# Rotary steps on VectorE straight from PSUM sums, and the indexer's columns as two held chunks and 80 float32 columns

## The chip, the cores and the metric

The kernel runs on one core of a Trainium2 chip. The time is the device time of one execution in microseconds (us); a comparison is made against runs of the kernel before on the same chip. PE is TensorE, DVE is VectorE, ACT is ScalarE, POOL is GpSimd, SP is the queue that issues the weight loads.

## The reference

One decoder layer on 256 rows of 2048 float32 values. What the change touches is the part from the first norm to the two attentions:

```python
h = _rmsnorm(x, g_pre_mix[l]) * (1.0 + sc1) + sh1        # sc1, sh1 = sections of silu(c) @ w_ada + b_ada
proj = h @ w_in[l]                                       # (256, 2048) @ (2048, 11344)
p_moba, p_dsa, p_qi, p_ki, p_wi, ga, gb = jnp.split(proj, split_pts, axis=-1)
q_idx = _rope(p_qi.reshape(B, T, IDX_HEADS, IDX_DIM))    # 16 heads x 64
k_idx = _rope(p_ki[:, :, None, :])[:, :, 0, :]           # 64 columns; p_wi has 16
ya = _moba_attention(_rope(qa), _rope(ka), va)...        # 8 heads x 128, causal softmax at this length
yb = _dsa_attention(_rope(qb), _rope(kb), vb, q_idx, k_idx, p_wi)...
# inside _dsa_attention: rel = relu(q_idx . k_idx); score = sum_h p_wi * rel * scale; keep the 64 largest per row
# _rope: [x1*cos - x2*sin, x2*cos + x1*sin] on the two halves of each head
```

Behind it come the gates, the two output projections, `w_o`, a second norm and a squared-ReLU MLP of width 8192; the change leaves these alone.

## The kernel before

**Tiles.** Rows are two tiles of 128 (`t` = 0, 1), the inner dimension 16 blocks of 128 (`k`). A matmul product of float32 accuracy is three float32r matmuls: each weight block `w` is cast on ACT to a high part `wh` (line 253), DVE subtracts to get the low part `wl` (line 254), and `products` (lines 268 to 270) issues hi x hi, hi x lo and lo x hi. Four `wh` and four `wl` buffers of 128x1024 exist, so at most two units of four k blocks are split ahead of PE; four raw `w` buffers (1 MB each) are loaded ahead by SP.

**The sweep.** The columns of `sc1` and `sh1` come as 2 x 16 rows of `w_ada`, each one a 1 MB load and a DVE dot product (line 443, name `w<-w,cB`). Each pair of them makes one more block `k` of the activations (`h_block`, lines 463 to 471). So that PE need not wait for all 16 blocks, `sweep()` visits the column chunks of `w_in` in turn and multiplies whatever blocks are ready: `iq0[2:4]` is chunk `iq0` over k = 2, 3. There are 13 chunks: `iq0`, `iq1`, `iq2` of 368 columns (16 x 64 query columns, 64 key columns and 16 weights of the indexer) and ten of 512 (`mq0` to `dk1`). Between visits a chunk's partial sums live in SBUF. For t = 0 DVE adds the visit's PSUM sums to them (line 487); for t = 1 ACT copies the old sums into PSUM before the visit (line 302) and copies them out behind it (line 485).

**PSUM.** Of eight banks four serve the products: `ps0` in two buffers, `ps1a` and `ps1b`. The other four are the pools `tp` and `sc` of two each, used by transposes and scores.

**Rotary steps.** `rope_piece` works on 128x512 sums in SBUF with four instructions: two of 128x256 (line 517), one product with cos (519), one add (520). For `mq`, `mk` it runs on POOL from `evict`, for `dq`, `dk` on POOL from `dsa_rope`, for the indexer on DVE from `indexer` once all of `iq2` is there.

**Beside the sums.** `beside()` runs a side line of work, a step at each unit (`tick`): the indexer's rotary steps, transposes (lines 545, 551), 16 heads of scores (560 to 569), then `topk` (eight rounds of MAX and MATCH_REPLACE, 578, 579), the eight MoBA heads (`heads`, lines 597 to 639) and `dsa_rope` together, then the DSA heads. The order on each engine is set by the framework's scheduler from program order and its own estimates; the queues then run in order.

Of the kernel before, what the change touches and what calls it, by code (L numbers as in the profile page):

```python
# [100 lines left out]
def sweep_units():  # L101

    return [(v[0], k, min(4, v[2] - k)) for v in sweep() if len(v) == 3 for k in range(v[1], v[2], 4)]


def column(name):
    return QI0 + IQ.index(name) * IDXW if name in IQ else COL[name]

# [45 lines left out]
def tile_layer(ctx: ExitStack, tc: tile.TileContext, xT, x, cT, ada, bT, gT, consts,  # L154
# [118 lines left out]
    open_to = [0, 0]  # L273
    kept = []

    def pair(keep=False):
# [4 lines left out]
        if keep and not kept:
            kept.extend(pm.tile([P, CW], F32, name=f"ps1{i}", tag=f"ps1{i}", bufs=1) for i in "ab")
        ps1 = kept[b] if keep else pm.tile([P, CW], F32, name="ps1", tag=f"ps1{'ab'[b]}", bufs=1)
        return [pm.tile([P, CW], F32, name="ps0", tag="ps0"), ps1]

    def chunk(dram, off, acts, k0, kt, cw, post, pre=None, by_t=0, weave=None, store=None, keep=False, back=None):
# [8 lines left out]
        def room():  # L295
            st["ps"] = pair(keep)
            b = turn[0]
            if back is None:
                open_to[b] = cw
            else:  # L300
                assert open_to[b] >= cw
                S.copy(st["ps"][1][:, :cw], back())
# [160 lines left out]
    def h_block(k):  # L463
# [6 lines left out]
        S.activation(h1[:, k, 0], hf, AF.Identity, bias=sh)  # L470
# [11 lines left out]
    def evict(name, first, last, t, ps):
        cw, dst = width(name), sums(name, t)
        if first or t == 1:
            S.copy(dst, ps[:, :cw])
        else:
            V.tensor_tensor(dst, ps[:, :cw], dst, ALU.add)
        if last:
            if t == NT - 1:
                ready.add(name)  # L490
            if name in ("mq0", "mk0", "mq1", "mk1"):
                rope_piece(dst, 4, HD // 2, C_COS, C_SIN, t, G)

    off = 0
    for name, k0, *k1 in sweep():
# [6 lines left out]
        chunk(w_in, off, lambda: h1, k0, k1[0] - k0, width(name),  # L502
              lambda t, ps, a=(name, k0 == 0, k1[0] == KT): evict(*a, t, ps), keep=True,
              back=k0 > 0 and (lambda name=name: sums(name, 1)) or None)
        off += P * (k1[0] - k0) * width(name)
# [3 lines left out]
    def rope_piece(xv, nh, half, c, s, t, eng):  # L509
        cos = con[:, c + t * half:c + (t + 1) * half]  # L510
        sin = con[:, s + 2 * t * half:s + 2 * (t + 1) * half].rearrange("p (b e) -> p b e", b=2)
        x3 = xv.rearrange("p (h e) -> p h e", e=half)
        x4 = xv.rearrange("p (h b e) -> p h b e", b=2, e=half)
        b = tmpt("rb")[:, :nh * 2 * half]
        b4 = b.rearrange("p (h b e) -> p h b e", b=2, e=half)
        for e in range(2):
            eng.tensor_tensor(b4[:, :, e, :], x4[:, :, 1 - e, :],
                              sin[:, e, None, :].to_broadcast([P, nh, half]), ALU.mult)
        eng.tensor_tensor(x3, x3, cos[:, None, :].to_broadcast([P, 2 * nh, half]), ALU.mult)
        eng.tensor_tensor(xv, xv, b, ALU.add)  # L520


    KI, WI = IH * ID, IH * ID + ID
# [519 lines left out]
```

## Time and profile before

| | us |
|---|---|
| median of three runs (lowest, highest) | 1513.4 (1513.02, 1515.19) |
| the profiled execution | 1518.06 |
| its span, first to last instruction | 1516.2 |
| PE busy in the span | 1461.5 |
| DVE / ACT / POOL busy | 1080.4 / 766.0 / 105.7 |

The profiled execution has 1.9 us around its span. PE is busy for 96% of the span, so the page's totals alone leave some 55 us of idle PE; the stretches in which they lie are shown below. A matmul row's duration overlaps the next one's, so the pace of PE is read from start to start.

### The profile page before, as it was taken

How to read it: one execution, taken by the hardware profiler on the slowest of the kernel's cores; microseconds unless marked ns; L12 is line 12 of the kernel's file. 1: busy time of each engine (PE TensorE's matmuls, PEld its weight loads, DVE VectorE, ACT ScalarE, POOL GpSimd, SP SyncE). 2: the span in 40 equal slices, each digit the busy share in tenths (PEclk: the TensorE clock that was granted, in tenths of full speed). 3: DMA queues.
4: the chain of work that ended last, by engine and by line, in shares of the span. 5: the costliest groups of instructions: out<-in, count | busy, mean ns of one | idle time of the engine just before them, and what ended most of it. 6: DMA issues, size and time to landing. Idle time of an engine off the chain costs nothing.

```text
span 1516.2 us, 18432 instructions
## 1 busy us (share of the span) xinstructions
PE 1461.5 (96%) x7094; PEld 1222.5 (81%) x7094; DVE 1080.4 (71%) x1330; ACT 766.0 (51%) x1105; POOL 105.7 (7%) x82
## 2 busy tenths in 40 slices
PE   6999999798899999999999999999999999999997
PEld 5777878576688888888888888888888888888885
DVE  6798997999976677888668765577655655466555
ACT  5665656454677544444555444444444443344443
POOL 0000000745700000000000000000000000000001
PEclk7999999899999999999999999999999999999999
DMA  8898987375677899877726666666655555555551
GB/s 306 303 319 311 336 311 282 134 252 210 244 273 262 294 336 348 333 302 287 302 70 240 233 240 250 249 249 240 245 208 195 189 176 194 194 191 195 185 192 67
DMA packets 56087, 369.49 MB, mean 244 GB/s; under 512 B 6432, under 2 KB 6688, under 8 KB 15808
## 3 DMA queue, kind: packets, MB, share of 16 engines
q1 hardware_dynamic: 55296, 366.15, 66.1%
q0 software_dynamic: 704, 2.18, 0.5%
q8 instruction: 55, 0.90, 0.2%
q14 instruction: 32, 0.26, 0.0%
HBM read 366.21 MB, written 2.10 MB: 243 GB/s over the span
## 4 chain that ended last, share of the span: by engine, by line
PE 83%; DVE 9%; DMA 3%; issue 2%; ACT 2%; DVEq 0%; ACTq 0%; SPq 0%
PE ps L269 17%; PE ps L270 17%; PE ps L268 17%; PE ps L351 16%; PE ps L353 8%; DVE wl L254 3%; DVE w L443 2%; DMA w<-in_w_in 1%; DMA w<-in_ada 1%; PE ps1b L269 1%; PE ps1b L270 1%; PE ps1a L270 1%; PE ps1a L269 1%; PE ps1b L268 1%; PE ps1a L268 1%
## 5 line engine op out<-in xcount | busy, mean ns | idle before, releaser
L254 DVE TENSOR_TENSOR wl<-w,wh 128x1024 fp32r<-128x1024 f32 (+3 forms) x516 | 613.1, 1196 | 341.7 <-ACT wh L253 340.8
L253 ACT CAST wh<-w 128x1024 fp32r<-128x1024 f32 (+3 forms) x516 | 521.1, 1014 | 531.3 <-PE ps L270 336.4
L351 PE MATMUL ps<-h,wh 128*128 128x512 f32 (+1 forms) x1056 | 359.5, 392 | 0.0
L353 PE MATMUL ps<-h,wl 128*128 128x256 f32 x1024 | 283.1, 281 | 0.0
L443 DVE SCALAR_TENSOR_TENSOR w<-w,cB 128x2048 f32<-128x2048 f32 x96 | 222.6, 2320 | 21.9 <-DMA w<-in_ada 21.7
L351 PEld LDWEIGHTS ps<-h,wh 128*128 128x128 f32 x1056 | 194.5, 188 | 46.5
L269 PE MATMUL ps<-wl,h 128*128 128x512 f32 (+1 forms) x528 | 208.6, 395 | 15.1 <-DVE wl L254 15.0
L268 PE MATMUL ps<-wh,h 128*128 128x512 f32 (+1 forms) x528 | 209.3, 396 | 7.5 <-ACT wh L253 7.3
L270 PE MATMUL ps<-wh,h 128*128 128x512 f32 (+1 forms) x528 | 206.3, 391 | 0.0
L268 PE MATMUL ps<-wh,f 128*128 128x512 f32 x512 | 199.4, 389 | 0.0
L269 PE MATMUL ps<-wl,f 128*128 128x512 f32 x512 | 199.3, 389 | 0.0
L270 PE MATMUL ps<-wh,f 128*128 128x512 f32 x512 | 199.2, 389 | 0.0
L353 PEld LDWEIGHTS ps<-h,wl 128*128 128x128 f32 x1024 | 191.5, 189 | 0.1
L269 PEld LDWEIGHTS ps<-wl,h 128*128 128x128 f32 x528 | 101.1, 192 | 38.9 <-DVE wl L254 20.9
L268 PEld LDWEIGHTS ps<-wh,h 128*128 128x128 f32 x528 | 100.7, 191 | 30.2 <-ACT wh L253 9.4
L270 PEld LDWEIGHTS ps<-wh,h 128*128 128x128 f32 x528 | 100.7, 191 | 18.1
L268 PEld LDWEIGHTS ps<-wh,f 128*128 128x128 f32 x512 | 96.1, 188 | 20.1
L270 PEld LDWEIGHTS ps<-wh,f 128*128 128x128 f32 x512 | 96.1, 188 | 20.0
L269 PEld LDWEIGHTS ps<-wl,f 128*128 128x128 f32 x512 | 96.1, 188 | 19.6
L960 POOL TENSOR_TENSOR y<-y,G 128x512 f32<-128x512 f32 x2 | 2.6, 1276 | 874.4 <-ACT junk L951 874.4
L268 PE MATMUL ps<-wh,o 128*128 128x512 f32 x128 | 50.1, 391 | 0.0
L270 PE MATMUL ps<-wh,o 128*128 128x512 f32 x128 | 49.8, 389 | 0.0
(225 smaller groups left out, 1552.7 us busy)
## 6 DMA issues: line engine op xcount, KB each, us to landing
w<-in_w_ff SPq DMA_DIRECT2D x128, 1024.0 KB, 4.8
w<-in_ada SPq DMA_DIRECT2D x96, 1024.0 KB, 5.7
w<-in_w_in SPq DMA_DIRECT2D x58, 1024.0 KB, 6.1
w<-in_w_o SPq DMA_DIRECT2D x16, 1024.0 KB, 5.5
w<-in_w_in SPq DMA_DIRECT2D x20, 768.0 KB, 6.3
w<-in_w_moba SPq DMA_DIRECT2D x8, 1024.0 KB, 6.9
w<-in_w_dsa SPq DMA_DIRECT2D x8, 1024.0 KB, 6.7
w<-in_w_in SPq DMA_DIRECT2D x11, 512.0 KB, 4.9
```

Source lines behind the costliest of these rows:

```text
L253: yield (lambda h=h, src=src: S.copy(h, src), lambda h=h, l=l, src=src: V.tensor_tensor(l, src, h.bitcast(F32), ALU.subtract))
L254: lambda h=h, l=l, src=src: V.tensor_tensor(l, src, h.bitcast(F32), ALU.subtract))
L268: TE.matmul(ps[t][:, :cw], hi, h, start=f, stop=False, skip_group_check=skip)
L269: TE.matmul(ps[t][:, :cw], hi, l, start=False, stop=False, skip_group_check=skip)
L270: TE.matmul(ps[t][:, :cw], lo, h, start=False, stop=e, skip_group_check=skip)
L351: TE.matmul(out, w, acts()[:, k, :, ts], start=k == 0 and ts.start == 0, stop=False)
L353: TE.matmul(out[:, 0], w, acts()[:, k, 0, ts], start=False, stop=k == KT - 1)
L443: V.scalar_tensor_tensor(w, w, 1.0, cB, ALU.mult, ALU.mult, accum_out=mod[:, i:i + 1])
L960: G.tensor_tensor(y, y, G2[(NC - 1) // 2][:, (NC - 1) % 2], ALU.mult)
```

## The change

1. The indexer's columns become two chunks of 512 (`iq0`, `iq1`) and 80 columns `ik`. `iq0` and `iq1` hold their sums over the whole sweep in the four banks of `tp` and `sc` (`hold`), with no copy out or in between visits. `ik` is done once, behind the last visit of `iq1`: 2 x 16 float32 matmuls of 80 columns from unsplit weights and a float32 copy of the activations, which `h_block` writes with one more ACT instruction per block into `sq`.
2. `ps0` gets fixed banks as `ps1` had (`ps0a`, `ps0b`). The t = 0 sums too are copied back into PSUM by ACT when the visit is four blocks long or the chunk's last; the DVE add stays for the others.
3. `rope` takes its input from PSUM where the sums are whole (`iq`, `ik`, `mq`, `mk`) and is three DVE instructions of 128x512, the first with a reversed step over the halves of a head. `dq`, `dk` go through the same on DVE from SBUF. POOL does no rotary step.
4. Small: the mask is added in the first score instruction, not in `topk`; the softmax's maximum comes out negated, so the 128x2 DVE instruction between maximum and exponential (line 612) goes.

```diff
-IDXW = 368
+KW = 80
+COL.update(iq0=QI0, iq1=QI0 + CW)
+IQ = ["iq0", "iq1"]
+BACK = 4
...
         def room():
-            st["ps"] = pair(keep)
-            b = turn[0]
-            if back is None:
-                open_to[b] = cw
-            else:
-                assert open_to[b] >= cw
-                S.copy(st["ps"][1][:, :cw], back())
+            st["ps"] = own() if own else pair(keep)
+            for t in range(NT):
+                if back[t]:
+                    S.copy(st["ps"][t][:, :cw], back[t]())
...
         S.activation(h1[:, k, 0], hf, AF.Identity, bias=sh)
+        S.activation(sq[:, k], hf, AF.Identity, bias=sh)
...
+    def rope(dst, src, nh, half, c, s, t):
+        cos = con[:, c + t * half:c + (t + 1) * half]
+        sin = con[:, s + 2 * t * half:s + 2 * (t + 1) * half].rearrange("p (b e) -> p b e", b=2)
+        b = tmpt("rb")[:, :nh * 2 * half]
+        V.tensor_tensor(b.rearrange("p (h b e) -> p h b e", b=2, e=half),
+                        src.rearrange("p (h b e) -> p h b e", b=2, e=half)[:, :, ::-1, :],
+                        sin[:, None].to_broadcast([P, nh, 2, half]), ALU.mult)
+        V.tensor_tensor(dst.rearrange("p (h e) -> p h e", e=half), src.rearrange("p (h e) -> p h e", e=half),
+                        cos[:, None, :].to_broadcast([P, 2 * nh, half]), ALU.mult)
+        V.tensor_tensor(dst, dst, b, ALU.add)
+    def evict(name, added, last, t, ps):
         if name in IQ:
+            if last:
+                rope(iq[:, t, IQ.index(name) * CW:(IQ.index(name) + 1) * CW], ps, 8, ID // 2, C_COSI, C_SINI, t)
+            return
+        dst = proj[name][:, t]
+        if last and name in ("mq0", "mk0", "mq1", "mk1"):
+            rope(dst, ps, 4, HD // 2, C_COS, C_SIN, t)
+        elif added:
+            S.copy(dst, ps)
         else:
+            V.tensor_tensor(dst, ps, dst, ALU.add)
...
+    def index_keys(off):
+        def mm():
...
+            for t in range(NT):
+                V.memset(ps[t][:, :KW], 0.0)
+                for k in range(KT):
+                    TE.matmul(ps[t][:, :KW], sq[:, k, t * P:(t + 1) * P], w[:, k], start=False, stop=k == KT - 1,
+                              skip_group_check=True)
+            for t in range(NT):
+                rope(kk2[:, t, 0], ps[t][:, :ID], 1, ID // 2, C_COSI, C_SINI, t)
+                S.copy(kk2[:, t, 1], kk2[:, t, 0])
+                V.tensor_scalar(wi[:, t], ps[t][:, ID:KW], (ID ** -0.5) * (IH ** -0.5), None, ALU.mult)
...
+        if name in IQ:
+            own = lambda name=name: hold(name)
+        elif k0:
+            back = [(lambda name=name, t=t: proj[name][:, t]) if t or k1 == KT or k1 - k0 >= BACK else None
+                    for t in range(NT)]
...
     def indexer():
-        while "iq2" not in ready:
+        while "ik" not in ready:
             yield
-        for t in range(NT):
-            for h0, hn in ((0, 8), (8, 8), (16, 1)):
-                rope_piece(iq[:, t, h0 * ID:(h0 + hn) * ID], hn, ID // 2, C_COSI, C_SINI, t, V)
...
-                V.tensor_tensor_reduce(e[:, c0:c0 + w], ps[:, c0:c0 + w], msk[:, c0:c0 + w], SCALE, GONE,
-                                       ALU.add, ALU.max, m[:, t:t + 1])
-            V.tensor_scalar(m[:, 0:2], m[:, 0:2], -1.0, None, ALU.mult)
+                V.tensor_tensor_reduce(e[:, c0:c0 + w], ps[:, c0:c0 + w], msk[:, c0:c0 + w], -SCALE, -GONE,
+                                       ALU.add, ALU.min, m[:, t:t + 1])
...
-                rope_piece(proj[n][:, t], 4, HD // 2, C_COS, C_SIN, t, G if ROPE == "pool" else V)
+                rope(proj[n][:, t], proj[n][:, t], 4, HD // 2, C_COS, C_SIN, t)
```

Line numbers move: the split's lines 253 and 254 become 249 and 250, the rotary step is lines 480, 483, 485, the dot product 437.

**On DVE at the end of the sweep.** `wl<-w,wh` is a weight split that PE waits for. Before, the indexer's rotary steps, done from SBUF, stand among the splits:

```order
L517 TENSOR_TENSOR rb<-p_iq,con 128x8x32 x2
L254 TENSOR_TENSOR wl<-w,wh 128x512
L519 TENSOR_TENSOR p_iq<-p_iq,con 128x512
L517 TENSOR_TENSOR rb<-p_iq,con 128x32 x2
L520 TENSOR_TENSOR p_iq<-p_iq,rb 128x512
L519 TENSOR_TENSOR p_iq<-p_iq,con 128x64
L517 TENSOR_TENSOR rb<-p_iq,con 128x8x32
L520 TENSOR_TENSOR p_iq<-p_iq,rb 128x64
L517 TENSOR_TENSOR rb<-p_iq,con 128x8x32
L254 TENSOR_TENSOR wl<-w,wh 128x1024
```

Now the splits of `mq0` and `mk0` stand ahead of the four steps of `iq` and the two of `ik` (`kk`, `wi`), and those of `mq0`, `mk0`, which POOL did, come between the next splits. From the last step of `iq1` on:

```order
L480 TENSOR_TENSOR rb<-ps0a,con 128x64
L485 TENSOR_TENSOR p_iq<-p_iq,rb 128x512
L483 TENSOR_TENSOR kk_98<-ps0a,con 128x64
L522 TENSOR_SCALAR wi<-ps0a 128x16
L485 TENSOR_TENSOR kk_98<-kk_98,rb 128x64
L480 TENSOR_TENSOR rb<-ps1a,con 128x64
L483 TENSOR_TENSOR kk_98<-ps1a,con 128x64
L522 TENSOR_SCALAR wi<-ps1a 128x16
L485 TENSOR_TENSOR kk_98<-kk_98,rb 128x64
L250 TENSOR_TENSOR wl<-w,wh 128x512
L250 TENSOR_TENSOR wl<-w,wh 128x1024
L480 TENSOR_TENSOR rb<-ps0b,con 128x512
```

All the indexer's rotary steps now stand in one row on DVE, with no split among them.

**On DVE in `topk`.** Before, rounds of MAX and MATCH_REPLACE follow each other, and the softmax's `st` instructions of the first MoBA heads (lines 612, 616) stand among them:

```order
L579 MATCH_REPLACE score<-m_2933,score 128x256
L612 TENSOR_SCALAR st<-st 128x2
L578 MAX m_2961<-score 128x8
L578 MAX m_2964<-score 128x8
L579 MATCH_REPLACE score<-m_2961,score 128x128
L579 MATCH_REPLACE score<-m_2964,score 128x256
L578 MAX m_2967<-score 128x8
```

Now `dq`'s and `dk`'s rotary steps stand between rounds, and splits too:

```order
L625 ISA e,st<-pss,con 128x256
L625 ISA st 128x1
L480 TENSOR_TENSOR rb<-p_dk_94,con 128x512
L250 TENSOR_TENSOR wl<-w,wh 128x1024
L630 RECIPROCAL st<-st 128x2
L483 TENSOR_TENSOR p_dk_94<-p_dk_94,con 128x512
L250 TENSOR_TENSOR wl<-w,wh 128x1024
L485 TENSOR_TENSOR p_dk_94<-p_dk_94,rb 128x512
```

**On ACT late in the sweep.** Before, one copy out (line 485) and one copy back (302) per visit stand between the casts:

```order
L302 COPY ps1a<-p_mk_90 128x512
L485 COPY p_mq_89<-ps1b 128x512
L302 COPY ps1b<-p_mv_91 128x512
L253 CAST wh<-w 128x1024 x2
L485 COPY p_mk_90<-ps1a 128x512
L302 COPY ps1a<-p_mv_92 128x512
```

Now there are two of each (lines 496 and 295), and the new copy of the activations (465):

```order
L295 COPY ps0b<-p_dq_95 128x512
L496 COPY p_dq_93<-ps1b 128x512
L295 COPY ps1b<-p_dq_95 128x512
L249 CAST wh<-w 128x1024 x2
L461 ACTIVATE s_86<-mod,b_sb 128x1
L464 ACTIVATE h_85<-hf,s_86 128x256
L465 ACTIVATE xs<-hf,s_86 128x256
L249 CAST wh<-w 128x1024 x2
L496 COPY p_dk_94<-ps0a 128x512
L295 COPY ps0a<-p_mq_87 128x512
```

The bank that a visit needs is free only behind both copies out and both copies back of the visit two before it.

More of the change, by code (lines that the diff above doesn't have):

```diff
@@ L92, in sweep @@
             worked = max(worked, loaded) + W_WORK * b
+            if n == IQ[-1] and usable == KT:
+                out.append(("ik", 0, KT))
         if shift is not None:
@@ L101, in sweep_units @@
 def sweep_units():
[L103 to L107 removed]
+    return [(v[0], k, min(n, v[2] - k)) for v in sweep() if len(v) == 3
+            for n in (KT if v[0] == "ik" else 4,) for k in range(v[1], v[2], n)]
 def constants():
@@ L281, in pair, with chunk @@
         if keep and not kept:
[L282 to L286, printed above, removed]
+            kept.extend([pm.tile([P, CW], F32, name=f"ps{t}{i}", tag=f"ps{t}{i}", bufs=1) for t in range(NT)]
+                        for i in "ab")
+        return kept[b] if keep else [pm.tile([P, CW], F32, name=f"ps{t}", tag=f"ps{t}{'ab'[b]}", bufs=1)
+                                     for t in range(NT)]
+    def chunk(dram, off, acts, k0, kt, cw, post, pre=None, by_t=0, weave=None, store=None, keep=False, back=(None, None), own=None):
         st = {}
@@ L312, in some @@
             def some(u, ts):
-                products(st["ps"], acts(), k0 + 4 * u, its[u]["parts"], cw, () if u else (0,) if back else range(NT),
-                         range(NT) if u == n - 1 else (), ts, keep)
+                opens = [t for t in range(NT) if u == 0 and not (back[t] or own and k0)]
+                products(st["ps"], acts(), k0 + 4 * u, its[u]["parts"], cw, opens,
+                         range(NT) if u == n - 1 else (), ts, keep or any(back))
             some(i, range(NT) if i < n - by_t else (0,))
@@ L482, in evict @@
[L482 to L485, printed above, removed]
-        else:
[L487 to L492, printed above, removed]
+    iq = cp.tile([P, NT, IH * ID], F32, name="p_iq", tag="p_iq")
+    kk2 = cp.tile([P, NT, 2, ID], F32, name="kk2")
@@ new lines, in hold @@
+    def hold(name):
+        if name not in held:
+            held[name] = [bank(tag, f"h_{name}") for tag in ("tp", "sc")]
+        return held[name]
+    def index_keys(off):
+        it = {}
+        def mm():
+            w = it["w"][:, :KT * KW].rearrange("p (k c) -> p k c", k=KT)
+            ps = it["ps"]
+            for t in range(NT):
[7 more added lines that the diff above has]
+                V.tensor_scalar(wi[:, t], ps[t][:, ID:KW], (ID ** -0.5) * (IH ** -0.5), None, ALU.mult)
+            ready.add("ik")
+        it.update(load=lambda: load(it, w_in, off, KT * KW), split=lambda: None, mm=mm,
+                  room=lambda: it.update(ps=pair(True)))
+        items.append(it)
@@ L501, in tile_layer @@
             continue
[L502 to L505, printed above, removed]
-    items.insert(24, dict(load=lambda: nc.sync.dma_start(con[:, P:], consts[:, P:]), split=lambda: None, mm=None))
[L509 to L523, printed above, removed]
+        k1 = k1[0]
+        if name == "ik":
+            index_keys(off)
+            off += P * KT * KW
+            continue
+        back, own = [None] * NT, None
+        if name in IQ:
+            own = lambda name=name: hold(name)
+        elif k0:
+            back = [(lambda name=name, t=t: proj[name][:, t]) if t or k1 == KT or k1 - k0 >= BACK else None
+                    for t in range(NT)]
+        chunk(w_in, off, lambda: h1, k0, k1 - k0, CW,
+              lambda t, ps, a=(name, [k0 == 0 or b is not None for b in back], k1 == KT): evict(a[0], a[1][t], a[2], t, ps),
+              keep=True, back=back, own=own)
+        off += P * (k1 - k0) * CW
+    items.insert(24, dict(load=lambda: nc.sync.dma_start(con[:, P:], consts[:, P:]), split=lambda: None, mm=None))
     BLK = ((0, 0, P), (1, P, T))
@@ L573, in topk @@
     def topk():
-        V.tensor_tensor(score, score, mask, ALU.add)
         for r in range(TOPK // 8):
```

34 lines of the change are left out of this document (9 added, 25 removed).

## The prediction

> **What bounds the kernel now.** I read the busy time by stretches first, then who waits for whom in the stretches where PE loses time, then the rows there. Columns: span, busy us and count of PE, PEld, DVE, ACT, POOL, granted clock, DMA share, GB/s.
>
> ```profile
> 0.00:40.00 40.00, 25.17 (x110) 22.44 (x111) 24.43 (x39) 22.05 (x36) 1.44 (x6) 0.74 0.81 305
> 40.00:260.00 220.00, 212.98 (x974) 177.89 (x973) 190.37 (x236) 139.24 (x227) 0.00 (x0) 0.99 0.86 311
> 260.00:300.00 40.00, 29.84 (x124) 23.99 (x123) 37.83 (x47) 17.52 (x26) 26.47 (x19) 0.87 0.45 159
> 300.00:360.00 60.00, 58.82 (x295) 45.16 (x294) 54.66 (x67) 32.42 (x51) 27.92 (x18) 1.00 0.73 262
> 360.00:420.00 60.00, 51.24 (x238) 40.68 (x237) 55.17 (x130) 36.20 (x83) 39.49 (x28) 0.91 0.55 203
> 420.00:520.00 100.00, 99.42 (x490) 82.27 (x489) 68.07 (x111) 70.03 (x126) 2.19 (x4) 1.00 0.75 273
> 520.00:1516.00 996.00, 983.97 (x4872) 830.05 (x4870) 649.81 (x706) 448.53 (x558) 8.19 (x8) 1.00 0.63 228
> ```
>
> Behind 420 PE never rests for long, so time won ahead of it is kept to the end. What PE loses is its idle time plus the lower clock on its busy time: 7.0 + 2.1 = 9 us in the sweep (40 to 260), 10.2 + 3.9 = 14 us in 260 to 300, 8.8 + 4.6 = 13 us in 360 to 420. In the last two POOL and DVE are busy together, and DVE has hardly a pause. The waits of 260 to 420 (total, times, longest):
>
> ```profile
> ACT e L614 <- DVE st L612: 12.3, 6, 4.8
> PE ps L269 <- DVE wl L254: 8.3, 2, 6.5
> PE ptp L624 <- ACT e L618: 7.5, 3, 4.2
> ```
>
> PE waits for DVE's splits, or for a softmax that waits for DVE. The long one, by time (start, us; POOL, DVE, PE):
>
> ```profile
> 275.18 1.25 POOL L519 TENSOR_TENSOR p_mq<-p_mq,con 128x512 f32<-128x512 f32 x1
> ...
> 268.10 0.68 DVE L520 TENSOR_TENSOR p_iq<-p_iq,rb 128x512 f32<-128x512 f32 x1
> 271.62 1.78 DVE L519 TENSOR_TENSOR p_iq<-p_iq,con 128x512 f32<-128x512 f32 x1
> 273.32 1.95 DVE L517 TENSOR_TENSOR rb<-p_iq,con 128x32 f32<-128x32 f32 x2
> 275.19 1.80 DVE L520 TENSOR_TENSOR p_iq<-p_iq,rb 128x512 f32<-128x512 f32 x1
> 278.91 1.21 DVE L254 TENSOR_TENSOR wl<-w,wh 128x1024 fp32r<-128x1024 f32 x1
> 280.05 0.68 DVE L519 TENSOR_TENSOR p_iq<-p_iq,con 128x512 f32<-128x512 f32 x1
> 280.65 1.21 DVE L254 TENSOR_TENSOR wl<-w,wh 128x1024 fp32r<-128x1024 f32 x1
> ...
> 273.11 0.39 PE L268 MATMUL ps<-wh,h 128*128 128x512 f32 x1
> 273.34 0.39 PE L268 MATMUL ps1a<-wh,h 128*128 128x512 f32 x1
> 280.18 0.80 PE L269 MATMUL ps<-wl,h 128*128 128x512 f32 x1 [6.46 <-DVE wl L254]
> ```
>
> The same DVE instruction (L519, L520) takes 0.68 us with POOL at rest and 1.8 beside a POOL rotary step. The price over the whole region is seen in groups of equal shape (count, busy us, mean ns), first 260 to 420, then 420 to 600:
>
> ```profile
> L254 DVE TENSOR_TENSOR wl<-w,wh 128x1024 fp32r<-128x1024 f32 x36 | 52.5, 1473 | 7.0 <-ACT wh L253 7.0
> L443 DVE SCALAR_TENSOR_TENSOR w<-w,cB 128x2048 f32<-128x2048 f32 x12 | 30.6, 2550 | 1.4 <-DMA w<-in_ada 1.4
> L612 DVE TENSOR_SCALAR st<-st 128x2 f32<-128x2 f32 x8 | 4.7, 593 | 0.0
> ...
> L254 DVE TENSOR_TENSOR wl<-w,wh 128x1024 fp32r<-128x1024 f32 x58 | 70.7, 1223 | 33.1 <-ACT wh L253 32.8
> L443 DVE SCALAR_TENSOR_TENSOR w<-w,cB 128x2048 f32<-128x2048 f32 x23 | 52.7, 2289 | 11.0 <-DMA w<-in_ada 10.8
> L612 DVE TENSOR_SCALAR st<-st 128x2 f32<-128x2 f32 x8 | 1.3, 164 | 0.0
> ```
>
> 36 x 0.25 + 12 x 0.26 + 8 x 0.43 = 15.6 us of DVE time that only POOL's neighbourhood costs, the slowed rotary steps not counted.
>
> **The parts of the change.** Prices:
>
> ```profile
> 263.41 0.33 PE L268 MATMUL ps<-wh,h 128*128 128x368 f32 x1
> 263.58 0.33 PE L269 MATMUL ps<-wl,h 128*128 128x368 f32 x1
> 7.67 1.02 PE L419 MATMUL pss<-ones,xs 128*128 128x1 f32 x8 [0.52 <-DVE xs L413]
> 358.44 0.82 PE L606 MATMUL pss<-qk 128*128 128x128 f32 x4
> ...
> L419 PE MATMUL pss<-ones,xs 128*128 128x1 f32 x28 | 4.9, 303 | 1.8 <-DVE xs L413 1.8
> L487 DVE TENSOR_TENSOR p_iq<-ps,p_iq x15: 530/535/543, 69.7 to 264.6; 128x368 f32<-128x368 f32 x15
> L487 DVE TENSOR_TENSOR p_mq<-ps,p_mq x9: 679/687/691, 77.9 to 294.1; 128x512 f32<-128x512 f32 x9
> ...
> L470 ACT ACTIVATE h<-hf,s x16: 503/507/512, 19.1 to 250.3; 128x256 fp32r<-128x256 f32 x16
> L302 ACT COPY ps1a<-p_dk 128x512 f32<-128x512 f32 x5 | 3.0, 591 | 0.1
> L253 ACT CAST wh<-w 128x1024 fp32r<-128x1024 f32 x50 | 51.4, 1048 | 18.2 <-DMA w<-in_w_in 9.5 <-DVE p_mq L487 3.5 <-PE ps1b L270 3.0
> ```
>
> *PE.* 3 x 16 x 2 x 3 = 288 matmuls of 368 columns at 0.17 us start to start (49.0) go; 192 of 512 at 0.23 (44.2) and 32 float32 ones come. A float32 matmul shows as two instructions: line 419 stands for 14 in the program and 28 in the trace. Even with one column eight of them take 1.02 us; without the last one's own 0.30, (1.02 - 0.30) / 7 = 0.10 from start to start, with it 0.13. Four of line 606, two of 128 and two of 256 columns, take 0.82, at most 0.2 each. Eighty columns stand nearer one than 192, so I take 0.11: 64 x 0.11 = 7.1, at most 12.8. The first of them needs no split, only the load, so PE can go on there while DVE is late. Sum +2.3 on PE's path (+2.3 to +8.0).
>
> *Start.* ACT is what PE waits for there: a cast of 1024 columns instead of 736 and a second 0.51 us instruction per activation block lie ahead of the first products: +0.7 (0 to +1.8).
>
> *Sweep, 40 to 260.* DVE loses 15 adds of 0.535 and, by the order, 20 of 41 adds of 0.687: 22 of its 190 us. ACT loses 36 copies of 368 columns (0.47 each by the duration of a 128x512 copy scaled, 16.9) and gains 40 copies of 0.59 (65 + 77 against 41 + 61 in the order) and 16 of 0.51: +15 us. The nine us of PE's loss here come where a dot product waits for its load and the splits queue behind it; DVE's relief shortens that queue but not the load, so I take -2 (-8, nearly all of it, to +5, if ACT's work delays visits). SP issues 67 weight loads where 73 were, of the same bytes in all; DMA's share of 0.45 and 0.55 in the two bad stretches leaves room for an earlier start of each.
>
> *End of the sweep (260 to 300).* I walk the new order with 0.60 us from start to start for a 128x512 instruction (280.05 to 280.65 above), 0.2 for the small ones, 1.14 for a split. From PE's start on the last visit of `iq0`: `iq0` ends at 4.1, `iq1` at 6.9, `ik` at 14.0, `mq0` at 16.8, `mk0` at 18.2; their splits are all ahead. DVE, in order, does the four `iq` steps (7.2) from 4.1 to 11.3, then its head waits for `ik` on PE, with the splits of `mq1` and `mk1` queued behind; PE has `mq0` and `mk0`, 4.2 us, to go on with. The `ik` steps end at 14.6, the two splits at 16.4, `mq0`'s and `mk0`'s steps (7.2) and a split of `mk1` from 17 to 25.4. `mq1` waits for the bank that `mq0`'s step reads and two copies back (0.5), the transposes of `mk0`'s keys for its add (0.6), `mk1` for bank and copies (0.5), `mv0` and `mv1` for splits behind scores and steps (0.4, 0.3): some 2.3 us, short ones, which cost little clock. With 1 us for clock, 14 becomes 3.3: -10.7 (-13 to 0). What POOL did here in 26.5 us costs DVE 8 x 3 x 0.60 = 14.4; what makes room for it is that the indexer's steps and the splits no longer run at half pace, and that DVE's last t = 0 adds go to ACT.
>
> *`topk` and MoBA heads (360 to 420).* DVE gains 8 steps of three, 24 x 0.60 = 14.4 us, and loses line 612 (4.7), the mask add and most of the 15.6 above. It stays full from `topk` on. A round of both tiles is two MAX (the row below) and two replacements of the same shapes, some 1.2 us; between two splits now lie at most 8 to 10 us of rounds, steps and a 2.3 us dot product, where the four split buffers hold 48 x 0.23 = 11 us of PE's work at most. Walking these rows PE waits 0.7, 1.5, 2.5, 0.3, 3.0 and 0.3: 8.3, against 8.8 idle now. But the 4.2 us wait below goes: line 612 stood behind rounds while its exponential and PE waited. The many small waits cost less clock, say 1.5 instead of 4.6: -3.4 (-12 to +4.4).
>
> ```profile
> 363.89 0.61 DVE L578 MAX8 m<-score 128x8 f32<-128x128 f32 x2
> 367.41 0.35 DVE L612 TENSOR_SCALAR st<-st 128x2 f32<-128x2 f32 x1
> 371.19 0.47 PE L624 MATMUL ptp<-con,e 128*128 128x128 f32 x1 [4.18 <-ACT e L618]
> ```
>
> *ACT behind the sweep and late in it.* A visit of four blocks is 24 x 0.23 = 5.5 us of PE; ACT has two casts (2.1), four copies (2.4) and half a microsecond or more of score activations or of a new activation block (0.51 twice): 5.0 to 5.5. Hardly any slack is left in some ten visits, and a copy back that comes late costs PE what it is late: I take 0.16 each, +1.6 (0 to +19, a rival below). In 420 to 520 the missing line 612 is worth -0.6.
>
> Sum: +0.7 - 2 + 2.3 - 10.7 - 3.4 + 1.6 - 0.6 = -12.1. The profiled execution took 1518.06, 4.7 above the median of the runs; against it 1506, against the median 1513.4 it gives 1501.3.
>
> [...]
>
> **The rivals.**
>
> *A: DVE is relieved more (1490).* If without POOL the splits stay ahead in `topk` too, 360 to 420 falls to 3 us of loss (-10) and the sweep to 4 (-5): -12.1 - 6.6 - 3, and -1.6 from ACT, make -23.3. For it: 22 us less in the sweep, POOL's 97 us gone. Against it: DVE has no pause from `topk` on.
>
> *B: POOL's cover is lost (1514).* The rotary steps were hidden work; in rows they delay splits. `topk` then loses 4.4 more, the end of the sweep wins only 6.5, the sweep nothing: +4.4 - 6.5 + 2.3 + 0.7 = +1. For it: 14.4 us go onto a DVE with 55 busy of 60.
>
> *C, slower: ACT's copies come onto the path (1518).* Twenty-four t = 0 sums are copied out and back by ACT in line with t = 1, where DVE added them beside it: 1.18 us per visit, 28 us if all of it delays PE. Two thirds, 19 us in place of 1.6, give +5. It decides from 14 us on, half of the visits. For it: the 5.0 to 5.5 against 5.5 above. Against it: a bank is needed only one visit later, `iq` visits need no copies, and ACT was busy 139 of 220 us.
>
> *D: the reversed step is slow.* No row shows it. 20 wide instructions at double their 0.60 would add 12 us at DVE's fullest: 1513. [...]
>
> **How the numbers follow.** Forecast 0.60 (its own range 1494 to 1508), A 0.16, B 0.10, C 0.08, D 0.06. About 0.2%, 3 us, is what a measurement of this kernel can tell from no change. Faster than 1510: 0.57 of the forecast, A's 0.16, 0.03 each of B and D: 0.79. Same: 0.02 of the forecast, 0.04 of B, 0.03 of D: 0.09. Slower: C's 0.08, 0.03 of B, 0.01 of the forecast: 0.12. The time is 1501. The range 1488 to 1515 takes in A, B and D, and leaves out the greater part of C above, and below it the case that neither stretch nor the sweep loses anything any more.
>
> **What would show it.** Right: no POOL work before the last microseconds; wide splits at 1.22 us throughout; the 6.5 us wait for `wl` gone, no wait over 3.5 us between 260 and 420; some 7 us of 80-column matmuls. Wrong: `ps0a`/`ps0b` products waiting for ACT's line 295 (C); step instructions of line 480 over 0.8 us (D); waits for `wl` of 5 us and more beside the steps (B).

## The result and the profile after

The changed kernel takes 1489.42 us, median of 4 runs (1488.92 to 1490.39); the kernel before, run again beside it, takes 1514.3. The ratio is 0.9834, with a 95% interval of 0.9817 to 0.985: 25 us faster, twice the 12.1 us forecast. The profiled execution took 1490.39 us, its span 1488.6. Its busy time by stretches, with the columns of the prediction's first table:

```profile
0.00:40.00 40.00, 24.66 (x93) 20.57 (x94) 25.24 (x41) 20.30 (x30) 1.45 (x6) 1.00 0.83 306
40.00:260.00 220.00, 216.49 (x957) 176.66 (x956) 184.52 (x217) 151.78 (x243) 0.00 (x0) 1.00 0.88 318
260.00:300.00 40.00, 39.88 (x209) 30.65 (x209) 34.64 (x64) 24.70 (x44) 0.00 (x0) 1.00 0.44 158
300.00:360.00 60.00, 58.83 (x289) 45.91 (x288) 56.22 (x134) 40.99 (x80) 0.00 (x0) 1.00 0.63 228
360.00:420.00 60.00, 59.73 (x296) 49.89 (x295) 53.60 (x79) 40.03 (x78) 0.00 (x0) 1.00 0.86 314
420.00:520.00 100.00, 99.93 (x480) 83.25 (x479) 71.06 (x96) 63.28 (x105) 2.13 (x4) 1.00 0.82 304
520.00:1489.00 969.00, 956.10 (x4749) 807.09 (x4747) 628.08 (x687) 435.02 (x544) 8.18 (x8) 1.00 0.61 225
```

PE now rests 0.1 us in 260 to 300 (10.2 before) and 0.3 us in 360 to 420 (8.8 before), and the granted clock is 1.00 in both (0.87 and 0.91 before). POOL's column is empty from 40 to 420. DVE is no less full than before: 56.2 and 53.6 of 60 us in 300 to 360 and 360 to 420, where it was 54.7 and 55.2. So it is not DVE's busy time that fell; it is what PE has to wait for. The waits of PE that the view lists from 260 to 420, then from 40 to 260, in the changed kernel (engine, line, whom it waited for: total us, times, longest):

```profile
PE pss L621 <- ACT qk L614: 0.9, 1, 0.9
PE ps L265 <- DVE wl L250: 0.3, 1, 0.3
...
PE ps0b L265 <- DVE wl L250: 2.4, 4, 0.8
PE ps0b L264 <- ACT wh L249: 0.9, 1, 0.9
```

The same view of the kernel before, from 40 to 260, begins

```profile
PE ps L269 <- DVE wl L254: 4.2, 7, 1.7
PE ps L268 <- ACT wh L253: 2.7, 2, 1.5
```

The groups of 260 to 420 whose means stood in the prediction at 1473 and 2550 ns (count, busy us, mean ns):

```profile
L250 DVE TENSOR_TENSOR wl<-w,wh 128x1024 fp32r<-128x1024 f32 x43 | 51.7, 1219 | 6.6 <-ACT wh L249 6.6
L437 DVE SCALAR_TENSOR_TENSOR w<-w,cB 128x2048 f32<-128x2048 f32 x14 | 32.0, 2286 | 1.6 <-DMA w<-in_ada 1.6
```

Without POOL both have the duration that they had from 420 to 600 in the kernel before (1223 and 2289 ns); 0.25 and 0.26 us of each were its neighbourhood. Forty-three splits took less time here than 36 did before.

### The profile page after: what moved, and what is told of

Same layout as the page of the kernel before. It is cut to its first block, busy times and chain, and to the rows that moved or that the text cites. A ratio compares the mean times of both kernels' runs of the same rounds, so it can differ in the third digit from the quotient of the medians.

```text
span 1488.6 us, 18240 instructions
## 1 busy us (share of the span) xinstructions
PE 1455.6 (98%) x7062; PEld 1214.0 (82%) x7062; DVE 1053.4 (71%) x1312; ACT 776.1 (52%) x1118; POOL 11.8 (1%) x18
## 4 chain that ended last, share of the span: by engine, by line
PE 88%; DVE 7%; DMA 2%; ACT 1%; issue 1%; DVEq 0%; ACTq 0%
PE ps L345 16%; PE ps L265 16%; PE ps L266 16%; PE ps L264 16%; PE ps L347 8%; DMA w<-in_ada 2%; DVE w L437 2%; DVE wl L250 2%; PE ps0b L265 1%; PE ps0b L266 1%; PE ps1b L266 1%; PE ps1b L265 1%; PE ps0b L264 1%; PE ps1b L264 1%; PE h_iq L265 1%
## 5 line engine op out<-in xcount | busy, mean ns | idle before, releaser
L250 DVE TENSOR_TENSOR wl<-w,wh 128x1024 fp32r<-128x1024 f32 (+1 forms) x507 | 599.0, 1191 | 344.0 <-ACT wh L249 341.9
L249 ACT CAST wh<-w 128x1024 fp32r<-128x1024 f32 (+1 forms) x507 | 517.5, 1026 | 519.9 <-PE ps L266 339.7
L437 DVE SCALAR_TENSOR_TENSOR w<-w,cB 128x2048 f32<-128x2048 f32 x96 | 219.4, 2286 | 19.0 <-DMA w<-in_ada 18.9
L264 PE MATMUL ps<-wh,h 128*128 128x512 f32 x320 | 126.5, 398 | 0.0
L265 PE MATMUL ps<-wl,h 128*128 128x512 f32 x320 | 125.4, 392 | 0.5 <-DVE wl L250 0.3
L266 PE MATMUL ps<-wh,h 128*128 128x512 f32 x320 | 125.3, 392 | 0.0
L265 PEld LDWEIGHTS ps<-wl,h 128*128 128x128 f32 x320 | 60.1, 188 | 14.2 <-DVE wl L250 2.1
L266 PEld LDWEIGHTS ps<-wh,h 128*128 128x128 f32 x320 | 60.1, 188 | 12.2
L264 PEld LDWEIGHTS ps<-wh,h 128*128 128x128 f32 x320 | 59.9, 188 | 12.0 <-issue 0.3
L265 PE MATMUL ps<-wl,o 128*128 128x512 f32 x128 | 49.8, 389 | 0.0
```

What stands on the lines that cost most here:

```text
L249: yield (lambda h=h, src=src: S.copy(h, src), lambda h=h, l=l, src=src: V.tensor_tensor(l, src, h.bitcast(F32), ALU.subtract))
L250: lambda h=h, l=l, src=src: V.tensor_tensor(l, src, h.bitcast(F32), ALU.subtract))
L264: TE.matmul(ps[t][:, :cw], hi, h, start=f, stop=False, skip_group_check=skip)
L265: TE.matmul(ps[t][:, :cw], hi, l, start=False, stop=False, skip_group_check=skip)
L266: TE.matmul(ps[t][:, :cw], lo, h, start=False, stop=e, skip_group_check=skip)
L437: V.scalar_tensor_tensor(w, w, 1.0, cB, ALU.mult, ALU.mult, accum_out=mod[:, i:i + 1])
```

## The experiments

Each kernel was timed beside the kernel before on the same chip; the chips differ from one group of kernels to the next, so kernels of different groups are compared by their ratios, and a difference of ratios is turned into time with 1514 us. A wide split is one of 128x1024. Idle is PE's idle time in the stretch, from rows like those above.

| kernel | median us | ratio to before, 95% | idle 260-300 | 300-360 | 360-420 |
|---|---|---|---|---|---|
| before | 1514.3 | 1 | 10.2 | 1.2 | 8.8 |
| changed | 1489.4 | 0.9834 (0.9817-0.985) | 0.1 | 1.2 | 0.3 |
| all wide steps on POOL | 1510.5 | 0.9964 (0.9949-0.998) | 8.7 | 8.5 | 2.9 |
| dq, dk steps on POOL | 1499.9 | 0.9892 (0.9876-0.9909) | 0.1 | 8.8 | 2.4 |
| before, steps on DVE | 1503.4 | 0.9912 (0.9889-0.9935) | 5.0 | 0.3 | 4.0 |
| changed, POOL busy beside | 1516.2 | 1.0006 (0.9995-1.0016) | 3.7 | 7.6 | 8.0 |
| line 612, mask add back | 1490.3 | 0.9844 (0.9824-0.9865) | 0.1 | 2.0 | 0.3 |
| t = 0 sums added by DVE | 1490.3 | 0.9846 (0.9826-0.9867) | 0.5 | 2.7 | 0.3 |
| iq through shared banks | 1499.6 | 0.9891 (0.9867-0.9916) | 1.6 | 1.2 | 0.3 |
| steps on sums in SBUF | 1488.2 | 0.9826 (0.9806-0.9846) | 0.9 | 1.2 | 0.6 |
| topk in one piece | 1494.1 | 0.9866 (0.9848-0.9883) | 0.1 | 5.3 | 0.0 |
| early first split | 1488.7 | 0.9826 (0.981-0.9841) | 0.3 | 1.4 | 0.3 |
| SBUF steps, early split | 1486.0 | 0.9805 (0.9788-0.9821) | 1.0 | 1.2 | 0.5 |

### POOL's steps put back

```
 if last and name in ("mq0", "mk0", "mq1", "mk1"):
-    rope(dst, ps, 4, HD // 2, C_COS, C_SIN, t)
+    S.copy(dst, ps)
+    rope_piece(dst, 4, HD // 2, C_COS, C_SIN, t, G)
...
-    rope(proj[n][:, t], proj[n][:, t], 4, HD // 2, C_COS, C_SIN, t)
+    rope_piece(proj[n][:, t], 4, HD // 2, C_COS, C_SIN, t, G)
```

> The changed kernel with the sixteen wide steps of mq, mk, dq and dk on POOL again (sums copied out by ACT first, four POOL instructions a step); all else as changed. Theory N (neighbour): what cost time before was that DVE ran at half pace wherever POOL worked beside it. Theory H (fewer instructions): the gain comes from what DVE and ACT no longer have to do (15 + 20 adds, the copies of iq, line 612, the mask add), whoever runs the steps. N: 260 to 420 loses 20 us or more again (27 before, 6 after), wide splits there take 1.45 us, 1508 (1503 to 1514). H: 1492 (1488 to 1496).

Measured: 1510.5. Wide splits from 260 to 420 took 1.57 us in the mean, and PE waited 8.4 us for probabilities and 7.4 us for the indexer's scores. N holds; four fifths of the gain are gone. This kernel has another order of instructions on DVE too, so it does not part POOL's neighbourhood from the order; the kernel with POOL busy beside, below, does.

The second part of that diff alone (dq and dk):

> The changed kernel with only the eight steps of dq and dk on POOL; those of mq and mk stay on DVE. N: POOL is busy only from about 300 on, half of the POOL work of before, so the end of the sweep stays clean and the loss returns in 330 to 420 alone: 1499 (1494 to 1504). H: 1490 (1487 to 1493).

Measured: 1499.9, as N said. The first stretch in which POOL works lost PE time (2.4 us more went in 360 to 420), and the stretch where it doesn't stayed clean:

```profile
260.00:300.00 40.00, 39.88 (x195) 30.15 (x195) 32.87 (x57) 25.40 (x44) 0.00 (x0) 1.00 0.47 165
300.00:360.00 60.00, 51.22 (x245) 39.42 (x243) 57.12 (x113) 35.19 (x65) 26.69 (x18) 0.97 0.63 235
```

The other way round, the kernel before with its steps on DVE:

```
-ROPE = "pool"
+ROPE = "dve"
...
-    rope_piece(dst, 4, HD // 2, C_COS, C_SIN, t, G)
+    rope_piece(dst, 4, HD // 2, C_COS, C_SIN, t, V)
```

> The kernel before with its sixteen POOL steps issued on DVE instead, by the same four instructions each, and nothing else. N: the two bad stretches lose some 8 to 12 us instead of 27, the sweep's 9 to 13 stay: 1497 (1492 to 1503). H: DVE, already full from 260 to 420, gets 64 instructions more, some 36 us at 0.68 and 0.35 us, and nothing is taken from it: 1514 or more (1510 to 1525).

Measured: 1503.4, faster than before though DVE got all of POOL's instructions: 11 us by the medians, 13 by the ratio (10 to 17). Wide splits took 1.22 us. H's 1514 is out, but 1497 was too hopeful: 5.0 and 4.0 us of idle time stayed. So moving the steps is worth some 13 us in the old kernel, and the other 12 need the rest of the change. Of the 5.0 us, 4.0 are two waits for ACT's copies of old sums back into a bank (line 302), with half pace behind each, products of 128x512 0.43 us from start to start in place of 0.23:

```profile
PE ps1b L268 <- ACT ps1b L302: 2.1, 1, 2.1
PE ps1a L268 <- ACT ps1a L302: 1.9, 1, 1.9
```

### POOL busy beside, for nobody

```
 rope(dst, ps, 4, HD // 2, C_COS, C_SIN, t)
+idle_step(dst, 4, HD // 2, C_COS, C_SIN, t, G)   # POOL: 6 x 256 columns, two SBUF inputs each
...
 rope(proj[n][:, t], proj[n][:, t], 4, HD // 2, C_COS, C_SIN, t)
+idle_step(proj[n][:, t], 4, HD // 2, C_COS, C_SIN, t, G)
```

> The changed kernel, and after each of the sixteen wide steps on DVE POOL reads the same sums and tables once more, in six instructions of 256 columns with the same number of elements as a step, into a scratch row that nobody reads. DVE's and ACT's work is unchanged and no engine waits for POOL. Two parts of N come apart: if the pace of DVE beside POOL alone is the cost, 1502 (1496 to 1508) with splits of 1.4 us and more beside POOL. If the cost was that others waited for POOL's results (theory Q), 1490 (1487 to 1493), as by H.

Measured: 1516.2, 26 us worse than the changed kernel, 14 more than N's middle and beyond its range. In the two traces PE, ACT and DVE run the same instructions in the same order from the first to the last (but for one pair of score products on PE), and none of them waits for POOL. ACT was busy 776.9 us here and 776.1 in the changed kernel, DVE 1089.0 and 1053.4. So the pace of DVE beside POOL alone did this. That it cost more than N's middle may come from the amount: POOL was busy 126.3 us here, 105.7 in the kernel before; this was not tried. Groups of 260 to 420, then PE's largest entry of the waits there:

```profile
L250 DVE TENSOR_TENSOR wl<-w,wh 128x1024 fp32r<-128x1024 f32 x34 | 52.2, 1550 | 0.0
L437 DVE SCALAR_TENSOR_TENSOR w<-w,cB 128x2048 f32<-128x2048 f32 x10 | 27.1, 2709 | 0.0
...
PE ps L265 <- DVE wl L250: 10.6, 8, 2.0
```

By time (start, us), mk's steps beside POOL show which DVE instructions suffer:

```profile
287.45 0.68 DVE L480 TENSOR_TENSOR rb<-ps0a,con 128x512 f32<-128x512 f32 x1
288.05 0.67 DVE L483 TENSOR_TENSOR p_mk<-ps0a,con 128x512 f32<-128x512 f32 x1
288.19 1.55 POOL L495 TENSOR_TENSOR rx<-p_mk,con 128x256 f32<-128x256 f32 x2
288.64 0.67 DVE L480 TENSOR_TENSOR rb<-ps1a,con 128x512 f32<-128x512 f32 x1
289.24 1.05 DVE L485 TENSOR_TENSOR p_mk<-p_mk,rb 128x512 f32<-128x512 f32 x1
289.82 1.93 POOL L497 TENSOR_TENSOR rx<-p_mk,con 128x256 f32<-128x256 f32 x2
290.21 0.68 DVE L483 TENSOR_TENSOR p_mk<-ps1a,con 128x512 f32<-128x512 f32 x1
291.07 1.22 DVE L485 TENSOR_TENSOR p_mk<-p_mk,rb 128x512 f32<-128x512 f32 x1
```

Lines 480 and 483, with one input in PSUM, keep their 0.67 to 0.68 us; line 485, with both in SBUF, takes 1.05 and 1.22. In the means of 260 to 420 it is the same: of the 128x512 instructions in the steps of `mq`, `mk`, `dq` and `dk`, those with an input in PSUM take 674 to 684 ns, those with both in SBUF 860 to 1081, but for line 480 on `dq` with 680. One SBUF input is no shelter for every instruction, though: in the kernel before line 612, with its one input of 128x2 in SBUF, took 0.59 us in the mean of 260 to 420, where POOL worked, and 0.16 from 420 to 600, where POOL was busy for 2.2 us.

### The smaller parts, undone one at a time

The softmax chain and the mask:

```
-V.tensor_tensor_reduce(e.., ps.., msk.., -SCALE, -GONE, ALU.add, ALU.min, m[:, t:t + 1])
+V.tensor_tensor_reduce(e.., ps.., msk.., SCALE, GONE, ALU.add, ALU.max, m[:, t:t + 1])
+V.tensor_scalar(m[:, 0:2], m[:, 0:2], -1.0, None, ALU.mult)
...
 def topk():
+    V.tensor_tensor(score, score, mask, ALU.add)
```

> The changed kernel with the small softmax part undone: line 612's negation (8 to 16 times) and the mask's own addition to the scores are back on DVE, the steps stay where they are. Theory S (softmax chain): line 612 stood between a score's maximum and its exponential, for which PE waited 4.2 us in the kernel before; back, it brings 4 us or more of waits into 330 to 420: 1494 (1492 to 1497). By N line 612 takes 0.16 us without POOL beside it (0.59 with), some 2 us of DVE time in all that DVE can spare: 1490 (1488.5 to 1491.5).

Measured: 1490.3, as N said. The 4.2 us wait that the prediction hung on line 612 does not come back with it.

The t = 0 sums (this kernel leaves out, at the last visits of mq and mk, what the earlier visits had summed for t = 0):

```
-BACK = 4
+BACK = 99
...
-... if t or k1 == KT or k1 - k0 >= BACK else None
+... if t or k1 - k0 >= BACK else None
```

> The changed kernel with the t = 0 sums of mq to dk added by DVE at every visit, as before, and no longer copied back by ACT: by the order DVE has 39 adds of 0.687 us in place of 21 (+12.4 us), ACT 102 copies of 0.59 us in place of 142 (-23.6 us). If DVE's relief in the sweep is what halved the loss there (9 before, 6 after by starts of matmuls), the loss in 40 to 300 grows by 4 (2 to 7): 1493.5. If ACT's copies stood on PE's path instead (the prediction's rival C in the small), it falls by 1 to 3: 1487.5.

Measured: 1490.3, neither of the two. From 40 to 260 PE was busy 216.85 us (216.49 in the changed kernel) with DVE at 192.07 and ACT at 138.57. The run moves both loads at once, so the time alone shows only that DVE's relief by 18 adds and ACT's load by 40 copies together are worth nothing that can be measured. PE's waits part them somewhat: in that stretch it waited 2.9 us for splits (2.4 in the changed kernel) and 0.2 us for casts (0.9).

The held banks:

```
-if name in IQ:
-    own = lambda name=name: hold(name)
-elif k0:
-    back = [(lambda name=name, t=t: proj[name][:, t]) ...
+if k0:
+    back = [(lambda name=name, t=t: sums(name, t)) ...
```

> The changed kernel with the sums of iq0 and iq1 no longer held in four banks of their own between visits: they go through the two shared pairs of banks, copied out and back by ACT like every other chunk (by the order +28 copies of 0.59 us on ACT, 16.5 us, and +6 adds on DVE). If the held banks are what relieved the sweep, its loss grows from 6 to 9 or more and the banks cost waits at its end: 1494 (1491 to 1498). If ACT has the room (152 busy of 220 us), 1490 (1488.5 to 1491.5).

Measured: 1499.6, outside the range of either theory, and its executions fall into two groups, 1491.7 and 1493.0, and 1499.4 to 1501.7. The profiled one is of the upper group. DVE, ACT and PE by time:

```profile
258.15 0.68 DVE L480 TENSOR_TENSOR rb<-ps0b,con 128x512 f32<-128x512 f32 x1
259.34 0.68 DVE L483 TENSOR_TENSOR p_iq<-ps0b,con 128x512 f32<-128x512 f32 x1
...
260.58 0.58 ACT L295 COPY ps0b<-p_mq 128x512 f32<-128x512 f32 x1
...
261.22 0.50 PE L264 MATMUL ps0b<-wh,h 128*128 128x512 f32 x1 [3.29 <-ACT ps0b L295]
...
262.68 0.63 PE L266 MATMUL ps0b<-wh,h 128*128 128x512 f32 x1
263.11 6.95 PE L519 MATMUL ps0a<-w,xs 128*128 128x80 f32 x32
...
269.85 7.04 PE L519 MATMUL ps1a<-w,xs 128*128 128x80 f32 x32
```

The steps of iq1 read the shared bank `ps0b` until 260.0, only then can ACT copy `mq0`'s sums into it, and PE stands for 3.3 us. Behind that wait the 80-column matmuls stand 0.21 us apart where the changed kernel has 0.11: some 6.5 us more for the 64 of them. With banks of their own iq's steps hold up nobody. (The one wait of this kind in the changed kernel, up to 275.1, is 0.12 us.) This explains the upper group; that the lower group is free of the half pace is argued from its 8 us, not seen in a trace.

The form of the steps:

```
-rope(dst, ps, 4, HD // 2, C_COS, C_SIN, t)                 # 3 instructions on DVE, sums read in PSUM
+S.copy(dst, ps)
+rope_piece(dst, 4, HD // 2, C_COS, C_SIN, t)               # 4 instructions on DVE, in place in SBUF
```

> The changed kernel with its twenty wide steps on DVE in the old form: ACT copies the whole sums to SBUF first (12 copies more), and a step is four instructions in place (two halves of 256 at 0.42 us, then 512 at 0.68 twice) in place of three that read PSUM. If the form of the step is what the changed kernel has over the kernel before with DVE's steps (1503 against 1489), half of these 14 us comes back: 1496 (1493 to 1502). If it is the order and the indexer's shape, only 20 x 0.16 = 3 us of DVE time and 12 copies are added: 1491 (1489 to 1493).

Measured: 1488.2, ratio 0.9826: not slower than the changed kernel, against both theories. Reading whole sums from PSUM and reversing in one instruction buys nothing here; by itself that part of the change could have been left out. The indexer's new shape, two chunks of 512 and 80 columns in place of three of 368, was undone in no run.

### The rounds of topk in one piece

In the changed kernel `topk` (the rounds and the two mask instructions behind them) runs from 322.7 to 351.9 with seven splits in it; before, from 362.7 to 378.2, and from 359.6 to 372.4, 12.8 us, there is no split. DVE's splits, first of before, then of the changed kernel (an x2 row is two):

```profile
357.26 2.35 DVE L254 TENSOR_TENSOR wl<-w,wh 128x1024 fp32r<-128x1024 f32 x2
372.43 1.95 DVE L254 TENSOR_TENSOR wl<-w,wh 128x1024 fp32r<-128x1024 f32 x1
...
331.50 1.22 DVE L250 TENSOR_TENSOR wl<-w,wh 128x1024 fp32r<-128x1024 f32 x1
340.77 1.22 DVE L250 TENSOR_TENSOR wl<-w,wh 128x1024 fp32r<-128x1024 f32 x1
342.57 1.22 DVE L250 TENSOR_TENSOR wl<-w,wh 128x1024 fp32r<-128x1024 f32 x1
344.31 2.35 DVE L250 TENSOR_TENSOR wl<-w,wh 128x1024 fp32r<-128x1024 f32 x2
356.12 1.22 DVE L250 TENSOR_TENSOR wl<-w,wh 128x1024 fp32r<-128x1024 f32 x1
```

```
     V.match_replace(score[:, c0:c0 + w], m8, score[:, c0:c0 + w], GONE)
-    if r % 2:
-        yield
+yield                     # once, behind the last round
```

> The changed kernel with all eight rounds of topk issued in one piece: no split, dot product or step of another item between them. In the changed kernel's trace the rounds take 29.2 us with seven splits between them (15.5 us and two splits in the kernel before), the longest stretch without a split is 9.5 us, and the four split buffers hold 48 x 0.23 = 11 us of PE's work. Theory G (gap): PE waits only where a stretch without a split outlasts these 11 us. Packed, 13.2 us of rounds and what stands beside them make a stretch of 14 or more: PE waits 3 to 7 us once and some more is lost to the clock, 1495 (1492 to 1499). Rival: what counts is DVE's sum of work in 320 to 420, which is unchanged: 1490 (1488.5 to 1491.5).

Measured: 1494.1, as G said. One wait, by the timeline, and what follows it:

```profile
335.08 0.80 PE L265 MATMUL ps<-wl,h 128*128 128x512 f32 x1 [5.32 <-DVE wl L250]
335.67 0.63 PE L266 MATMUL ps<-wh,h 128*128 128x512 f32 x1
336.10 0.63 PE L265 MATMUL ps<-wl,h 128*128 128x512 f32 x1
...
342.34 0.39 PE L265 MATMUL ps<-wl,h 128*128 128x512 f32 x1
342.57 0.40 PE L266 MATMUL ps<-wh,h 128*128 128x512 f32 x1
```

A stretch of 14.8 us without a split (319.0 to 333.8) costs 5.3 us of waiting and, at 0.43 us from start to start until 341, some 2.7 us of half pace in this execution, the slowest of its four (1497.45); the changed kernel's stretches of 8.1 and 9.5 us cost 0.1 us each.

The length of the stretch is not all, though. With the t = 0 sums added by DVE, one of 9.6 us (321.3 to 330.9) costs 1.0 us. In the kernel before with its steps on DVE, the rounds and `dq`'s and `dk`'s steps leave 18.7 us without a split:

```profile
344.03 2.60 DVE L254 TENSOR_TENSOR wl<-w,wh 128x1024 fp32r<-128x1024 f32 x2
365.33 1.22 DVE L254 TENSOR_TENSOR wl<-w,wh 128x1024 fp32r<-128x1024 f32 x1
```

PE waits for none of the splits there. It runs the products that it has, then transposes and scores, and loses 3.0 us to four short waits for the softmax (361.1 to 366.3).

### A version faster than both

The largest loss left is the start, where PE waits 5.0 us for the first cast and 3.2 us for the first `wl`.

```
-for it in items[1:2 * FIRST]:
-    it["split"]()
+for i in (1, 2):
+    items[i]["split"]()
+items[4]["load"]()
+items[4]["split"]()
+items[3]["split"]()
...
-loads = splits = 2 * FIRST
+loads = splits = 2 * FIRST + 1
```

> The changed kernel with the first weight load's two splits ahead of the fourth dot product at the start, on DVE's queue (and that load right behind the four loads of the start). The start is the largest loss that is left, 18 of 31 us; PE waits 3.2 us there for the first wl, which stands behind two dot products of 2.29 us. If that wait bounds the start, 1 to 2 us are won: 1488 (1487 to 1489). If the second block's activations, which come 2.4 us later then, take its place, 1490 (1489 to 1491).

Measured: 1488.7, ratio 0.9826. The wait for `wl` fell from 3.2 to 0.4 us, but the next product waits 0.7 us for a cast; the gain of about 1 us lies within the interval. With the SBUF steps:

> The kernel with steps in four instructions on sums copied to SBUF (measured at 1488.2) together with the early first split. If both small gains are there and add, 1486.5 (1485.5 to 1487.5), faster than the changed kernel by 0.2%; if neither is more than noise, 1489.5 (1488.5 to 1490.5).

Measured: 1486.0, ratio 0.9805 (0.9788 to 0.9821), the fastest kernel of the study. Against the changed kernel's 0.9834 that is 0.3% by ratios that were measured on different chips and whose intervals overlap, so that it beats the kernel before is shown, that it beats the changed kernel is likely.

## Why the prediction was half right

**The direction and the mechanism held.** It was POOL's neighbourhood that made DVE late and DVE that made PE wait: taking POOL's steps away pays (13 us in the old kernel), putting them back costs (20 us), and POOL work that nobody needs costs as much (26 us). All that was said to show it came: no POOL work from 40 to 420, wide splits at 1.22 us, the 6.5 us wait gone, no wait over 3.5 us (0.9 is the longest), 7.1 us of 80-column matmuls. What happened is rival A: 1490 forecast, 1489.4 measured, with 0.3 us of loss in 360 to 420 where A had 3, and 3.5 in the sweep where A had 4. That A's number comes within 1 us is partly luck: by the two profiles the terms add up to 29.7 us (below) where A had 23.3, and 2.1 us of that are not placed and 2.8 are how far the profiled executions lie off their medians. The forecast's 1501 was 12 us too slow, outside its own case's 1494 to 1508. The step that failed is the price that the walk put on `topk`; the end of the sweep, priced 3 us too high, comes next.

**PE's term was right.** The 64 instructions of 80 columns begin 0.11 us apart, 257.4 to 264.4; DVE's wait for them was 2.1 us, 2.7 by the walk. Duration (least, median, most ns), first and last start:

```profile
L517 PE MATMUL ps0a<-w,xs x32: 230/275/275, 257.4 to 260.8; 128*128 128x80 f32 x32
L517 PE MATMUL ps1a<-w,xs x32: 275/275/275, 260.9 to 264.4; 128*128 128x80 f32 x32
```

**The start** was forecast at +0.7 and is +1.1 by its two waits (8.2 us against 7.1).

**The sweep, -2, measured -5.6** (9.1 of loss before, 3.5 after). Part of that is not the change's. The kernel before with its steps on DVE has the same instructions in the same order up to the end of the sweep, and lost less there, by the first table's columns:

```profile
40.00:260.00 220.00, 214.47 (x997) 180.88 (x996) 193.34 (x241) 142.98 (x233) 0.00 (x0) 1.00 0.87 316
```

That is 5.5 us against 9.1 for one program in two executions, so the change is worth between 2.0 and 5.6 in the sweep, and -2 is its lower end. The reason given, DVE's fewer adds, shows in no run: with 18 of them back, and ACT's copies gone, PE was busy 216.85 us against 216.49. The 15 adds of `iq` were not put back alone. With iq in the shared banks PE was busy 213.25 us there, 6.8 short, of which 2.1 are the wait for the bank before 260: the held banks are worth some 1 us of the sweep, and the wait at its end, for which the walk had no term.

**The end of the sweep, -10.7, measured -13.9** (14 to 0.1). The walk was right in its order and 2.2 us too pessimistic in its small waits: 0.12 us is left of the 2.3. The 1 us for the clock did not come either: the granted clock of the stretch is 1.00. That short waits cost little clock was the prediction's estimate, and not all do: behind waits of 1.2 and 0.5 us close together the kernel before has half pace (130.3 to 133.3).

**`topk` and MoBA heads, -3.4, measured -13.1** (13.4 to 0.3): the largest miss. The walk charged 8.3 us of waits to stretches of 8 to 10 us without a split, although it had put the work held in four split buffers at 11 us. For the splits behind the two longest stretches of `topk`, which end at 342.0 and 357.3, PE waited 0.09 and 0.12 us: they came just in time, not late. The packed rounds, 12.8 us without a split, stood in the kernel before and went with the new order; packed again in the changed kernel, they cost some 5 us. It is not the same wait, however. In the kernel before no wait of PE from 360 to 420 was for a split: 7.5 us were for probabilities (line 624, the row in the prediction's waits) and 1.2 for a score. The longest, 4.2 us, came while the softmax's instructions stood among the rounds, the others behind the rounds. Line 612 by itself has no part in it (put back: same time); what mattered, as far as the runs show, was that it stood behind packed rounds. How much of the 13.1 us is the order and how much POOL's pace was not separated.

**ACT's copies, +1.6, measured nothing**: PE's waits from 40 to 260 name no copy of line 295, and the one wait for it from 260 on is 0.12 us. Rival C is out. So is D: in 260 to 420 the reversed step takes what the others take (count, busy us, mean ns):

```profile
L480 DVE TENSOR_TENSOR rb<-ps0b,con 128x512 f32<-128x512 f32 x2 | 1.4, 684 | 0.4 <-PE ps0b L266 0.4
L480 DVE TENSOR_TENSOR rb<-p_dq,con 128x512 f32<-128x512 f32 x4 | 2.7, 686 | 0.0
L485 DVE TENSOR_TENSOR p_dq<-p_dq,rb 128x512 f32<-128x512 f32 x4 | 2.7, 681 | 0.0
```

Nor does an input in PSUM cost more than one in SBUF: line 480 takes 684 ns from `ps0b` and 686 from `p_dq` here, and in the kernel before it was 0.687 us with one input in PSUM (line 487) against 0.68 with both in SBUF (line 520). B is out as well: its lost cover would show as waits for `wl` of 5 us; one of 0.3 us came.

The sum by the two profiles is -5.6 in the sweep, -13.9, -13.1, -0.5 in 420 to 520, +2.3 for PE and +1.1 for the start, -29.7 against -27.6 of span; 2.1 us are not placed. The profiled execution of before lies 3.8 us above the median of its runs (1518.06 against 1514.3), that of the changed kernel 1.0 above its own, which is the rest of the way to 24.9. Why the build spreads the rounds now and packed them before was not tried. The steps' place on DVE is not it: with `dq` and `dk` on POOL splits still stand between the rounds (325.8 to 343.8), and in the kernel before with its steps on DVE none do.

## What to carry to other kernels

Before an elementwise step is given to POOL because it is idle, ask which instructions of DVE run beside it: here, beside POOL, wide splits went from 1.22 to 1.55 us and dot products from 2.29 to 2.71, both with two SBUF inputs, and the steps that POOL "hid" cost more than DVE doing them itself (13 us in the old kernel, 20 in the changed one). To judge whether DVE is too full, do not add up its work but find the stretches without the instruction that PE needs next, and compare each with the work that PE has in hand when it begins. The length alone does not tell: 7.2 us without a split cost 6.5 us in the kernel before (271.7 to 278.9), 9.5 cost 0.1 in the changed kernel, and 18.7 no wait for a split in the one with its steps on DVE. A sum that a slow reader takes straight from PSUM needs a bank that no one else is waiting for: with iq in the shared banks PE stood for 3.3 us.
